# Sixteen column units of the input projection as eight pairs with seven quarter products each, in a stage ahead of the attention, and an attention with a lag of three head tiles

## The chip, the cores and the metric

The kernel runs on one core of a Trainium2 chip. The metric is device time in microseconds, taken as the median of several runs. The engines are TensorE (PE in the profile, with its weight loads as PEld), VectorE (DVE), ScalarE (ACT), GpSimd (POOL) and SyncE (SP, which issues most transfers here). Every engine takes its instructions in the order of the program.

## The reference

One layer of a streaming encoder, for 1024 prompt tokens and 64 sample tokens (1088 together, T in the code) with 1024 channels. Cut to what matters:

```python
h = rms_norm(x, norm_w) @ w_in                       # 1024 x 6144
sb_q, sb_k, sb_v, sb_z, cb_q, cb_k, cb_v, cb_z, g_sb, g_cb = split(h)
# stick-breaking attention, 8 heads of 64
w[t, s] = beta[t, s] * prod(1 - beta[t, j] for s < j < t)   # beta = sigmoid(q.k / 8)
o_sb = w @ v
# band attention: softmax(q.k / 8 + rel_bias) over 9 chunks of 64, q and k normalised per head
o_cb = softmax(...) @ v
b_sb = (o_sb * silu(sb_z)) @ w_proj_sb
b_cb = (o_cb * silu(cb_z)) @ w_proj_cb
y = x + (sigmoid(g_sb) * b_sb + sigmoid(g_cb) * b_cb) @ w_out
```

Keys and values of both branches are outputs too. All is float32. The kernel gets float32 accuracy out of a faster type: each operand is split into a high part and a low remainder, and a product is the sum of three: high by high, low by high, high by low.

## The kernel before

**Phase 1** (lines 150 to 408) normalises the input and transposes it into `xhl`, high and low parts with channels on partitions and tokens along the row. It then computes eight groups of 256 columns of the input projection (list `NB`) with tokens on partitions: the values of both branches and the queries and keys of the band branch. The matmuls are on line 357.

**Column units.** The other 32 blocks of 128 columns are units (`make_units`, line 120): stick-breaking keys and queries (4 + 4), the two SiLU gates (4 + 4), the two branch gates (8 + 8). `run_fill` (line 556) is a generator that issues one matmul of a unit at a time (line 563): for each of three chunks of tokens (384, 384 and 320) eight channel blocks by three products, 72 matmuls a unit. Weights of the next unit are split by `W.split`: `whi` on ACT (line 91), `wlo` on POOL (line 98). The results leave through `ev_k`, `ev_q`, `ev_silu` and `ev_act`. Keys and queries go by transfers from SBUF to SBUF to the place where the attention reads them (`place_k`, `place_q`).

**Attention** (lines 692 to 905) walks over 144 head tiles (`seq`): stick-breaking then band, four head pairs each, per pair the sample tile (t = 8) and eight tiles of 128 queries, two heads each. One step of the loop has these parts, in this order on PE: scores of head tile i (`qk`, lines 725 and 726), half of the step's fillers (`fill`, from `run_fill`), outputs of a finished pair of tiles (`av`, line 817), transposes of the weights of head tile i - LAG (`tr`, line 777), the other half of the fillers. ACT makes two sigmoids of the scores (`kp`, line 728, and `be`, line 729). DVE makes the weights of head tile i (`mid`): a scan of products over the keys (line 745) and a multiplication (line 746). The transposed weights leave PSUM by ACT (line 786) and DVE (line 788) in turn. The number of fillers of a step follows its number of keys; 22 units' worth less 48 matmuls are spread over the stick-breaking steps, and 746 matmuls over the band steps, the last of which belong to the first branch projection (`proj_units`, line 661). Ahead of the first step stand two units and 48 matmuls (the lead-in, lines 858 to 860).

**Merge and output** (phases 4 and 5) do the rest of the projections (line 661), the gated merge and the output projection (lines 986 to 992).

What sets the order is the program's text: the fillers' number per step, the lag, and how many buffers each tile has (`kp` 2, `be` 3, two PSUM tiles for transposes, three for scores).

## Time and profile before

| | us |
|---|---|
| median of three runs | 1036.61 (1036.37 to 1039.8) |
| span of the profiled execution | 1034.6 |
| phase 1 after its start, 19 to 231 us | 212 |
| lead-in, 231 to 267 us | 36 |
| stick-breaking attention, 267 to 633 us | 366 |
| band attention, 633 to 870 us | 237 |
| merge and output, 870 to 1035 us | 165 |

The span runs from the first to the last instruction of one profiled execution; that execution's own time is not given apart from it. The page has the engines' busy times, the chain of work that ended last, groups of instructions and DMA issues; an answer by stretches has the busy time of each engine in a stage, an answer on waits what an engine stood idle for. A matmul's duration in the trace covers its way through the array, and neighbours overlap; the distance between two starts is what it costs in a row.

### The profile page before, as it was taken

The numbers are of one execution on the slowest core, as the hardware profiler recorded it, in microseconds if no ns is written. First come the engines' busy times: TensorE is split into PE (matmuls) and PEld (weight loads), VectorE is DVE, ScalarE is ACT, GpSimd is POOL, SyncE is SP. The second block draws the span as 40 slices with busy tenths as digits, with TensorE's granted clock in tenths as the row PEclk, the third lists the DMA queues.
The fourth block names the chain that finished last, engine by engine and source line by source line (L and its number), as shares of the span: only waits on it lengthen the run. The fifth ranks groups of instructions, "written<-read, shape, count | busy, mean of one in ns | idle before, by whom it ended". The sixth has DMA issues, their size and how long they took to land.

```text
span 1034.6 us, 19354 instructions
## 1 busy us (share of the span) xinstructions
PE 1014.8 (98%) x7412; PEld 968.4 (94%) x7412; DVE 543.9 (53%) x1069; ACT 418.7 (40%) x942; POOL 255.2 (25%) x277
## 2 busy tenths in 40 slices
PE   6999999999999999999999999999999999999998
PEld 5999999999999989999999999998988898999998
DVE  5416656402476556657655645565557685674111
ACT  5534443212454435444444454444445433552000
POOL 3227666202221111212121111101103211453110
PEclk9999999999999999999999999999999999999999
DMA  7654453745547323723384354665576834554322
GB/s 237 213 187 151 163 191 128 267 136 165 160 112 192 96 69 102 206 60 95 92 211 122 107 144 131 165 169 161 162 204 185 224 92 139 187 163 149 101 93 71
DMA packets 159660, 155.23 MB, mean 150 GB/s; under 512 B 23184, under 2 KB 144912, under 8 KB 159440
## 3 DMA queue, kind: packets, MB, share of 16 engines
q1 hardware_dynamic: 142800, 136.17, 44.2%
q10 hardware_dynamic: 16768, 17.83, 5.7%
q8 instruction: 58, 0.95, 0.4%
q14 instruction: 34, 0.28, 0.1%
HBM read 90.77 MB, written 49.81 MB: 136 GB/s over the span
## 4 chain that ended last, share of the span: by engine, by line
PE 91%; SPq 3%; DMA 2%; DVE 1%; ACT 1%; issue 1%; POOL 0%; ACTq 0%; DVEq 0%
PE acc L563 33%; PE acc L357 18%; PE acc L661 9%; PE o L817 7%; PE pt L777 6%; PE z L726 3%; PE z L725 3%; PE acc L992 3%; PE acc L991 3%; PE acc L990 3%; SPq L49 2%; DMA wrawx<-in_w_in_dram 1%; PE pk L301 1%; PE pt L229 1%; DMA d_ccbT<-hc 1%
## 5 line engine op out<-in xcount | busy, mean ns | idle before, releaser
L563 PE MATMUL acc<-xh,whi 128*128 128x384 f32 (+1 forms) x768 | 255.5, 333 | 0.1
L563 PE MATMUL acc<-xh,wlo 128*128 128x384 f32 (+1 forms) x768 | 255.3, 332 | 0.0
L563 PE MATMUL acc<-xl,whi 128*128 128x384 f32 (+1 forms) x768 | 254.8, 332 | 0.0
L98 POOL TENSOR_TENSOR wlo<-wraw,whi 128x1024 fp32r<-128x1024 f32 x51 | 127.6, 2501 | 440.2 <-ACT whi L91 386.1
L563 PEld LDWEIGHTS acc<-xh,wlo 128*128 128x128 f32 x768 | 144.8, 189 | 1.3
L563 PEld LDWEIGHTS acc<-xl,whi 128*128 128x128 f32 x768 | 144.5, 188 | 1.3
L563 PEld LDWEIGHTS acc<-xh,whi 128*128 128x128 f32 x768 | 144.5, 188 | 1.2 <-ACT sg L550 0.3
L745 DVE TENSOR_TENSOR_SCAN kp<-kp,imp 64x576 f32<-64x576 f32 (+8 forms) x72 | 110.6, 1536 | 5.1 <-ACT kp L728 5.1
L735 ACT ACTIVATE be<-be,sm 128x640 f32<-128x640 f32 (+5 forms) x72 | 50.8, 706 | 106.6 <-DVE sm L731 106.4
L728 ACT ACTIVATE kp<-z 128x384 f32<-128x384 f32 (+6 forms) x112 | 53.8, 480 | 97.3 <-PE z L726 87.6
L777 PE MATMUL pt<-ident,be 128*128 128x128 f32 (+2 forms) x608 | 88.8, 270 | 0.9 <-DVE wT L788 0.6
L786 ACT ACTIVATE wT<-pt 128x512 f32<-128x512 f32 (+3 forms) x104 | 52.9, 509 | 82.5 <-PE pt L777 81.6
L788 DVE COPY wT<-pt 128x256 f32<-128x256 f32 (+3 forms) x104 | 46.0, 442 | 70.3 <-PE pt L777 69.9
L777 PEld LDWEIGHTS pt<-ident,be 128*128 128x128 f32 (+2 forms) x608 | 68.7, 139 | 11.6 <-issue 7.1
L357 PE MATMUL acc<-whi,xh 128*128 128x256 f32 x256 | 75.2, 296 | 0.0
L357 PE MATMUL acc<-wlo,xh 128*128 128x256 f32 x256 | 71.7, 282 | 0.0
L357 PE MATMUL acc<-whi,xl 128*128 128x256 f32 x256 | 71.5, 281 | 0.0
L357 PE MATMUL acc<-whix,xh 128*128 128x256 f32 x256 | 70.9, 279 | 0.0
L357 PE MATMUL acc<-whix,xl 128*128 128x256 f32 x256 | 70.6, 278 | 0.0
L91 ACT ACTIVATE whi<-wraw 128x1024 fp32r<-128x1024 f32 x52 | 55.0, 1059 | 38.4 <-DVE y L996 35.8
L357 PE MATMUL acc<-wlox,xh 128*128 128x256 f32 x256 | 70.5, 277 | 0.0
L746 DVE TENSOR_TENSOR be<-be,kp 64x576 f32<-64x576 f32 (+8 forms) x72 | 62.3, 865 | 8.8
(157 smaller groups left out, 2168.7 us busy)
## 6 DMA issues: line engine op xcount, KB each, us to landing
wraw<-in_w_in_dram SPq DMA_DIRECT2D x40, 512.0 KB, 4.9
sq<-hl SPq DMA_DIRECT2D x32, 192.0 KB, 4.5
sq<-d_qT SPq DMA_DIRECT2D x32, 192.0 KB, 3.6
xt<-in_x_prompt_dram SPq DMA_DIRECT2D x8, 512.0 KB, 5.6
wrawx<-in_w_in_dram SPq DMA_DIRECT2D x8, 512.0 KB, 4.3
d_kT<-hl SPq DMA_DIRECT2D x8, 512.0 KB, 4.7
d_qT<-hl SPq DMA_DIRECT2D x8, 512.0 KB, 4.8
ks<-d_kT SPq DMA_DIRECT2D x16, 256.0 KB, 4.6
```

What stands on the lines that cost most here:

```text
L91: A.activation(h, raw, AF.Copy)
L98: (eng or G).tensor_tensor(out=l, in0=raw, in1=h[:].bitcast(F32), op=OP.subtract)
L357: TE.matmul(ps, x, w, start=m == 0, stop=m == len(steps) - 1)
L563: TE.matmul(ps[:, :b - a], w[:, k], xk(x, k)[:, a:b], start=k == 0 and n == 0, stop=k == KT - 1 and n == 2)
L661: TE.matmul(ps[:, :n], w[:, p, cw], g[:, a:e], start=p == 0 and m == 0, stop=p == NPAIR - 1 and m == 2)
L728: A.activation(kp[:r, x:y], z[:r, :m], AF.Sigmoid, scale=-0.125)
L735: A.activation(be[:r, :n], be[:r, :n], AF.Exp, bias=kp[:r, j:j + 1], scale=-1.0, accum_out=kp[:r, 2:3])
L745: V.tensor_tensor_scan(kp[:r, n - 1::-1], kp[:r, n - 1::-1], im[:, ::-1], 0.0, op0=OP.mult, op1=OP.add)
L746: V.tensor_tensor(out=be[:r, :n], in0=be[:r, :n], in1=kp[:r, 1:n + 1], op=OP.mult)
L777: TE.transpose(pt[:kr, x, :r], be[:r, kb * 128:kb * 128 + kr], ident[:r, :r])
L786: A.activation(w[:, sl:sl + m, q0:q0 + r], pt[:, :m, :r], AF.Copy)
L817: TE.matmul(o[hd * 64:hd * 64 + 64, c0:c1], vv[:kr, kb, hd * 64:hd * 64 + 64], wT[b, p, j, hd, s // 4][:kr, s % 4, c0:c1], start=si == 0, ...
```

## The change

Sixteen units (stick-breaking keys and queries, both SiLU gates) leave the attention. They are taken as eight pairs of 128 + 128 columns. For a pair the weights are a 2 by 2 block matrix (two halves of the channels, two units) and the input is one too (two halves of the channels, two halves of the tokens). The eight products of quarters are replaced by seven products of sums and differences of quarters. The tokens in `xhl` are put in two halves of 544 (512 prompt and 32 sample tokens each), which are worked on in chunks of 256 and 288 columns.

- Phase 1: the sums of input quarters (`make_t`) are made one per token tile during the last weight groups, and split again into high and low parts. The groups of `NB` stand in another order, the key transposes follow one tile later, and the cache transposes are three tiles apart.
- New stage (lines 530 to 646 of the kernel after): 56 products, each 24 matmuls. The sums of weights are made on DVE (`presum`), their high parts on ACT and low parts on POOL (`prep`), five products ahead. The products accumulate in six PSUM banks, and DVE adds the intermediate sums. Keys and queries are stored to DRAM, and the attention loads them from there, as it did for the band branch.
- Attention: a lead-in of 144 filler matmuls with the first loads between them, 504 fillers in the stick-breaking steps, 684 in the band steps. The lag is three head tiles, `kp` has three buffers and `be` four. In the stick-breaking part three of four groups of transposed weights leave by ACT. The gated outputs that the first projection reads (`make_og`) are split in small steps between fillers.

```diff
+    pairs = []
+    for p in (0, 2):
+        pairs += [("k", 512 + 128 * p, p), ("q", 128 * p, p)]
+    for p in (0, 2):
+        pairs += [("silu", 1536 + 128 * p, d_z["sb"][p:p + 2]), ("silu", 3584 + 128 * p, d_z["cb"][p:p + 2])]
+    units = [("ev_act", 4096 + 128 * j, (AF.Sigmoid, d_g["sb"][j])) for j in range(KT)]
+    units += [("ev_act", 5120 + 128 * j, (AF.Copy, d_g["cb"][j])) for j in range(KT)]
...
+            def sub(a, b, k):
+                d = pool.tile([128, HF], F32, name="d")
+                V.tensor_tensor(out=d, in0=x(0, *a[:1], k, a[1]), in1=x(0, *b[:1], k, b[1]), op=OP.subtract)
+                V.tensor_tensor(out=d, in0=d, in1=x(1, *a[:1], k, a[1]), op=OP.add)
+                V.tensor_tensor(out=d, in0=d, in1=x(1, *b[:1], k, b[1]), op=OP.subtract)
+                return d
+            def less(h, c, d, k):
+                e = pool.tile([128, HF], F32, name="d")
+                V.tensor_tensor(out=e, in0=x(0, h, k, c), in1=d, op=OP.subtract)
+                V.tensor_tensor(out=e, in0=e, in1=x(1, h, k, c), op=OP.add)
+                return e
+            def sums_of(k):
+                d = sub((0, 1), (0, 0), k)
+                yield 0, k, d
+                d = less(1, 1, d, k)
+                yield 1, k, d
+                yield 3, k, less(1, 0, d, k)
+                yield 2, k, sub((1, 1), (0, 1), k)
...
+            if s == 1:
+                sums[1] = total(r1[:, :, b], r2[:, :, b], OP.add)
+                sums[2] = total(sums[1], r1[:, :, a], OP.subtract)
+            elif s == 4:
+                sums[3] = total(r1[:, :, a], r1[:, :, b], OP.subtract)
+                load_raw(2 * i + 3)
+            else:
+                sums[4] = total(r2[:, :, a], sums[2], OP.subtract)
...
+            A.activation(t[:, 0], src, AF.Copy)
+            G.tensor_tensor(out=t[:, 1], in0=src, in1=t[:, 0].bitcast(F32), op=OP.subtract)
...
+        LEAD, HB = 5, 4
...
+            h = up.tile([128, 2, 288], F32R, name="hl", bufs=HB)
+            A.activation(h[:, 0, :n], src[:, :n], AF.Copy)
+            V.tensor_tensor(out=h[:, 1, :n], in0=src[:, :n], in1=h[:, 0, :n].bitcast(F32), op=OP.subtract)
+            p = arg + w
+            dst = (d_kT if kind == "k" else d_qT)["sb"][p]
+            soon(0, lambda: stores(rdma, half, c, h[:, :, :n], dst[:]))
...
+        right = [lambda s: xhl[s][0][:, :, 0:HF], lambda s: tms[1][s], lambda s: tms[0][s],
+                 lambda s: xhl[s][1][:, :, 0:HF], lambda s: tms[2][s], lambda s: tms[3][s],
+                 lambda s: xhl[s][1][:, :, HF:T]]
+        BANK = "1231223"
...
+            for s in range(7):
+                n = 7 * i + s
+                prep(n + LEAD)
+                presum(n + LEAD + 1)
+                if n + LEAD == 7 * len(pairs) + 2:
+                    W.split(("u", 0))
+                if n + LEAD == 7 * len(pairs) + 1:
+                    load_unit(1)
+                step()
+                w = blk.pop(n)
+                for c, (a, b) in enumerate(XC):
+                    m = b - a
+                    if s < 3:
+                        bank[BANK[s], c] = psB.tile([128, 512], F32, name=f"b{BANK[s]}{c}")
+                    ps = bank[BANK[s], c]
+                    for k in range(4):
+                        for e, (hl_, x) in enumerate(((0, 0), (0, 1), (1, 0))):
+                            TE.matmul(ps[:, :m], w[:, hl_, k], right[s](x)[:, k, a:b], start=s < 3 and k == 0 and e == 0,
+                                      stop=k == 3 and e == 2, skip_group_check=s > 2)
+                    if s == 0:
+                        s1[c] = up.tile([128, 288], F32, name="s1")
+                        A.activation(s1[c][:, :m], ps[:, :m], AF.Copy)
+                    elif s in (1, 4):
+                        u = up.tile([128, 288], F32, name="u2" if s == 1 else "u3")
+                        (u2 if s == 1 else u3)[c] = u
+                        V.tensor_tensor(out=u[:, :m], in0=ps[:, :m], in1=s1[c][:, :m], op=OP.add)
+                    elif s == 3:
+                        emit(i, 0, 0, c, ps, True)
+                    elif s == 5:
+                        V.tensor_tensor(out=s1[c][:, :m], in0=ps[:, :m], in1=s1[c][:, :m], op=OP.add)
+                        emit(i, 1, 0, c, s1[c], False)
+                    elif s == 6:
+                        V.tensor_tensor(out=u2[c][:, :m], in0=ps[:, :m], in1=u2[c][:, :m], op=OP.add)
+                        emit(i, 0, 1, c, u2[c], False)
+                if s == 4:
+                    for c, (a, b) in enumerate(XC):
+                        m = b - a
+                        V.tensor_tensor(out=u3[c][:, :m], in0=bank["3", c][:, :m], in1=u3[c][:, :m], op=OP.add)
+                        emit(i, 1, 1, c, u3[c], False)
...     def fill(n):
+        n += owed[0]
+        owed[0] = 0
...
-        be = am.tile([128, NP], F32, name="be", bufs=3)
+        be = am.tile([128, NP], F32, name="be", bufs=4)
...
-            kp = ax.tile([128, NP + 2], F32, name="kp", bufs=2)
+            kp = ax.tile([128, NP + 2], F32, name="kp", bufs=3)
...
-                if flip[0] % 2:
+                if flip[0] % 2 or b == "sb" and flip[0] % 4:
...
-    load_v("sb", 0)
-    until(1)
-    fill(48)
-    FP = 170
-    n_sb = 72 * FILL_SB - 48
-    n_cb = 72 * (len(units) - 2 - FILL_SB) + FP
+    load_k("sb", 0, 1)
+    for f in (lambda: load_q("sb", 0, 3), lambda: load_k("sb", 0, 0), lambda: load_q("sb", 0, 0),
+              lambda: load_v("sb", 0), lambda: None, lambda: None):
+        fill(24)
+        flush()
+        f()
+    FP = 180
+    n_sb = 72 * 7
+    n_cb = 72 * (len(units) - 9) + FP
...
-    LAG = 2
+    LAG = 3
```

Three places show how the instructions stand. The first is PE at the end of phase 1. Before, the first unit follows (`xh`, `xl` are the input's high and low parts, `whi`, `wlo` the weights'):

```order
L357 MATMUL acc<-whix,xh_132 128x256
L357 MATMUL acc<-whix,xl_134 128x256
L357 MATMUL acc<-wlox,xh_132 128x256
L563 MATMUL acc<-xh_131,whi 128x384
L563 MATMUL acc<-xl_133,whi 128x384
L563 MATMUL acc<-xh_131,wlo 128x384
```

and after, the first product follows (`b` are its banks; high and low weights now share a tile):

```order
L451 MATMUL acc<-whix,xh_140 128x256
L451 MATMUL acc<-whix,xl_142 128x256
L451 MATMUL acc<-wlox,xh_140 128x256
L622 MATMUL b_3284<-xh_139,whi 128x256
L622 MATMUL b_3284<-xl_141,whi 128x256
L622 MATMUL b_3284<-xh_139,whi 128x256 x2
L622 MATMUL b_3284<-xl_141,whi 128x256
```

In the place of 72 matmuls a unit of 384 and 320 columns stand 24 a product of 256 and 288; the whole program has 2304 of line 563 before, and 1344 of line 622 and 1152 of line 759 after.

The second place is DVE beside the products of a key pair, in the new stage (`u` and `s` are the intermediate sums, `kf` a copy of the keys for their transposes, `ws` the sums of weights, `hl` the high and low parts):

```order
L387 TENSOR_TENSOR ws<-wraw 128x512
L387 TENSOR_TENSOR ws<-ws,wraw 128x512
L567 TENSOR_TENSOR hl<-b_3284,hl 128x256
L576 COPY kf<-b_3284 128x256
L567 TENSOR_TENSOR hl<-b_3299,hl 128x288
L576 COPY kf<-b_3299 128x288
L630 TENSOR_TENSOR u_3437<-b_3319,s_3297 128x256
L630 TENSOR_TENSOR u_3451<-b_3334,s_3312 128x288
L642 TENSOR_TENSOR u_3437<-b_3356,u_3437 128x256
L567 TENSOR_TENSOR hl<-u_3437,hl 128x256
```

Before, DVE had for a key unit only these two operations per chunk, here of the unit at the lead-in:

```order
L505 COPY kf<-acc 128x384
L495 TENSOR_TENSOR hl<-acc,hl 128x384
L505 COPY kf<-acc 128x384
L495 TENSOR_TENSOR hl<-acc,hl 128x384
L505 COPY kf<-acc 128x320
L495 TENSOR_TENSOR hl<-acc,hl 128x320
```

The evacuations moved out of the attention, and sums of weights and of products came to them.

The third place is DVE in the stick-breaking attention, at the tiles of 512 and 640 keys of the second head pair. Before:

```order
L745 SCALAR_TENSOR_TENSOR kp<-kp,imp 128x512
L746 TENSOR_TENSOR be<-be,kp 128x512
L788 COPY wT<-pt 128x3x128
L745 SCALAR_TENSOR_TENSOR kp<-kp,imp 128x512
L746 TENSOR_TENSOR be<-be,kp 128x512
L505 COPY kf<-acc 128x384
L495 TENSOR_TENSOR hl<-acc,hl 128x384
L745 SCALAR_TENSOR_TENSOR kp<-kp,imp 128x640
L746 TENSOR_TENSOR be<-be,kp 128x640
```

and after (the scan is the row with `kp` and `imp`, the copy of transposed weights the row with `wT`):

```order
L952 SCALAR_TENSOR_TENSOR kp<-kp,imp 128x512
L953 TENSOR_TENSOR be<-be,kp 128x512
L1027 TENSOR_TENSOR zt<-o,zt 128x256
L952 SCALAR_TENSOR_TENSOR kp<-kp,imp 128x512
L953 TENSOR_TENSOR be<-be,kp 128x512
L952 SCALAR_TENSOR_TENSOR kp<-kp,imp 128x640
L953 TENSOR_TENSOR be<-be,kp 128x640
L952 SCALAR_TENSOR_TENSOR kp<-kp,imp 128x640
L953 TENSOR_TENSOR be<-be,kp 128x640
L995 COPY wT<-pt 128x4x128
```

Scans and multiplications stand closer together: the units' evacuations are gone from between them, and of the copies of transposed weights 24 are left of 50.

426 lines of the change are left out of this document (259 added, 167 removed).

## The prediction

> **What bounds the kernel now.** I read the page's head and the chain first, then the busy time by stage, then what TensorE (PE) waited for.
>
> ```profile
> span 1034.6 us, 19354 instructions
> PE 1014.8 (98%) x7412; PEld 968.4 (94%) x7412; DVE 543.9 (53%) x1069; ACT 418.7 (40%) x942; POOL 255.2 (25%) x277
> PE 91%; SPq 3%; DMA 2%; DVE 1%; ACT 1%; issue 1%; POOL 0%; ACTq 0%; DVEq 0%
> 19.00:231.00 212.00, 210.76 (x1800) 209.79 (x1799) 94.33 (x202) 80.47 (x198) 94.08 (x101) 1.00 0.54 181
> 231.00:267.00 36.00, 35.62 (x219) 35.30 (x217) 6.83 (x12) 9.29 (x15) 8.11 (x6) 1.00 0.67 179
> 267.00:633.00 366.00, 365.88 (x2464) 343.90 (x2465) 220.47 (x261) 169.34 (x382) 60.48 (x91) 1.00 0.43 121
> 633.00:870.00 237.00, 234.90 (x1698) 213.16 (x1697) 149.06 (x469) 106.51 (x254) 38.00 (x34) 1.00 0.60 169
> 870.00:1035.00 165.00, 158.96 (x1191) 158.32 (x1190) 64.97 (x115) 42.51 (x78) 46.80 (x29) 1.00 0.41 130
> PE pt L229 <- DVE xn L218: 8.1, 2, 7.5
> PE acc L357 <- ACT whi L91: 2.2, 1, 2.2
> ```
>
> PE is busy 98% of the span and is 91% of the chain that ended last. The five stages (columns: length, then PE, weight load, VectorE (DVE), ScalarE (ACT), GpSimd (POOL), clock, DMA) are phase 1, the lead-in, the stick-breaking attention, the band attention, and the merge with the output projection. PE idles 0.1 us in the 366 us of the stick-breaking attention; what it waited for is mostly the start (8.1 us). So PE work that goes away shortens the kernel one for one, until another engine of the same stage is late. The nearest is DVE: 220 us of 366 there.
>
> **What the change takes from PE.** "Busy" overlaps neighbours, so the cost of one matmul is its spacing from start to start.
>
> ```profile
> 226.05 0.29 PE L357 MATMUL acc<-whix,xh 128*128 128x256 f32 x1
> ...
> 228.85 0.29 PE L357 MATMUL acc<-whix,xh 128*128 128x256 f32 x1
> 230.23 0.34 PE L563 MATMUL acc<-xh,whi 128*128 128x384 f32 x1
> ...
> 238.38 0.34 PE L563 MATMUL acc<-xh,wlo 128*128 128x384 f32 x1
> 238.56 0.49 PE L522 MATMUL pt<-ident,kf 128*128 128x128 f32 x3
> 238.80 0.39 PE L563 MATMUL acc<-xh,whi 128*128 128x320 f32 x1
> 239.03 0.30 PE L563 MATMUL acc<-xl,whi 128*128 128x320 f32 x1
> ...
> 242.25 0.31 PE L563 MATMUL acc<-xh,wlo 128*128 128x320 f32 x1
> 639.55 0.29 PE L725 MATMUL z<-kss,sqs 128*64 128x288 f32 x1
> ...
> 639.95 0.29 PE L726 MATMUL z<-kss,sqs 128*64 128x288 f32 x1
> ```
>
> A 384-column matmul takes (238.38 - 230.23) / 47 = 0.1734 us, a 320-column one (242.25 - 239.03) / 22 = 0.1464 us, a 256-column one (228.85 - 226.05) / 24 = 0.117 us, and a 288-column one (639.95 - 639.55) / 3 = 0.133 us. A column unit of before is 48 matmuls of 384 and 24 of 320 columns: 8.32 + 3.51 = 11.84 us. Sixteen of them are **189.4 us**. Of after, each of 8 pairs has 7 products of 12 matmuls of 256 and 12 of 288 columns: 12 x (0.117 + 0.133) = 3.0 us a product, 56 products, **168.0 us**. The change takes 21.4 us from PE. The key transposes become 40 instead of 36, at (238.80 - 238.56) / 3 = 0.08 us: 0.3 us, left out.
>
> The rule that speaks against this: the Trainium skill, page "TensorE: Matmul & The Clock Gate", section "Back-to-back issue gap", gives for a stream of weight load and matmul about 81 ns at 128 columns and 131 ns at 512. An estimate between these two figures of that page of the Trainium skill (98, 102, 106 and 114 ns at 256, 288, 320 and 384 columns) has the old units at 128 us and the products at 134 us, so that the change would cost 6 us. The trace does not agree with it (0.1734 us at 384 columns), and the sum goes by the trace.
>
> **What it adds on the other engines, stage by stage.**
>
> Phase 1. The 16 sums of input quarters are 40 DVE operations and 16 low-part subtractions of 544 columns, and 16 ACT copies; they stand one sum per token tile beside the last three weight groups. By the 576-column multiplication of 0.75 us quoted below the 56 operations are 42 us of DVE. Their cover is 19 tiles or more of 24 matmuls, 2.8 us each by the spacing, 53 us, in a phase where DVE is busy 94 of 212 us. I take 0; if the cover is gone, the second product waits for its quarter, some us once. The new order of weight groups, the later key transposes and the spread cache transposes touch waits that PE does not show; 0, bounds -1 and +2.
>
> The new stage. Each product needs a 512-column copy on ACT and a 512-column subtraction on POOL, each pair four sums on DVE, and evacuations.
>
> ```profile
> L98 POOL TENSOR_TENSOR wlo<-wraw,whi 128x1024 fp32r<-128x1024 f32 x51 | 127.6, 2501 | 440.2 <-ACT whi L91 386.1
> wraw<-in_w_in_dram SPq DMA_DIRECT2D x40, 512.0 KB, 4.9
> d_kT<-hl SPq DMA_DIRECT2D x8, 512.0 KB, 4.7
> ```
>
> POOL: half of 2.5 us, 7 times, 8.8 of a pair's 21 us. DVE has some 24 operations a pair of 0.3 to 0.6 us (the copies and evacuations below are 0.38 to 0.48 us), some 11 us. Weights are prepared five products (15 us) ahead, loads land in 4.9 us. PE accumulates again in a bank that DVE has just read: the sixth product starts its first half 1.6 us (12 x 0.133) after the fifth ended its own, and DVE's addition takes about 0.4 us. The staging ring has four tiles, so a store must land within about two products (6 us) against 4.7 us. All hides; what is left is the entry (weights that wait for memory of phase 1: 0.5 us of copy and 1.3 us of subtraction against the 6 us that two prepared products cover) and the exit. I take **+2 us**, bounds 0 and +12 (1.5 us a pair).
>
> The lead-in has 144 matmuls (24 us) instead of the first units. In it the queue on SP loads five pieces, each 4 to 5 us after issue, one after another; keys and queries now come back from DRAM, and the store of a filler that waits for ACT stands ahead of the next load. 24 us cover about 20: 0, bounds 0 and +5.
>
> The stick-breaking attention is where it is decided. It loses 1032 of 1536 filler matmuls (1032 x (2 x 0.1734 + 0.1464) / 3 = 169.6 us) and 27 transposes, so PE needs 366 - 169.6 - 2 = **194 us**. What DVE needs:
>
> ```profile
> L745 DVE TENSOR_TENSOR_SCAN kp<-kp,imp 64x576 f32<-64x576 f32 (+8 forms) x72 | 110.6, 1536 | 5.1 <-ACT kp L728 5.1
> L746 DVE TENSOR_TENSOR be<-be,kp 64x576 f32<-64x576 f32 (+8 forms) x71 | 61.1, 860 | 8.7
> L788 DVE COPY wT<-pt 128x256 f32<-128x256 f32 (+3 forms) x50 | 23.8, 476 | 54.5 <-PE pt L777 54.3
> L820 DVE TENSOR_TENSOR zt<-o,zt 128x256 f32<-128x256 f32 (+1 forms) x19 | 7.3, 383 | 41.9 <-PE o L817 32.6 <-PE acc L563 5.5 <-DMA zt<-d_zsb 3.7
> 345.44 2.28 DVE L745 TENSOR_TENSOR_SCAN kp<-kp,imp 128x1024 f32<-128x1024 f32 x1
> 347.86 1.23 DVE L746 TENSOR_TENSOR be<-be,kp 128x1024 f32<-128x1024 f32 x1
> 358.66 2.40 POOL L98 TENSOR_TENSOR wlo<-wraw,whi 128x1024 fp32r<-128x1024 f32 x1 [9.43 <-ACT whi L91]
> 359.63 2.64 DVE L745 TENSOR_TENSOR_SCAN kp<-kp,imp 64x576 f32<-64x576 f32 x1
> 362.37 0.75 DVE L746 TENSOR_TENSOR be<-be,kp 64x576 f32<-64x576 f32 x1
> 364.49 1.34 DVE L745 TENSOR_TENSOR_SCAN kp<-kp,imp 64x576 f32<-64x576 f32 x1
> 369.76 0.42 DVE L745 TENSOR_TENSOR_SCAN kp<-kp,imp 128x128 f32<-128x128 f32 x1
> 370.31 0.29 DVE L746 TENSOR_TENSOR be<-be,kp 128x128 f32<-128x128 f32 x1
> ```
>
> A step of scan and multiplication takes 2.42 + 1.23 = 3.65 us at 1024 keys and 0.55 + 0.29 = 0.84 us at 128, so 0.44 us + 3.14 ns a key; over the 72 steps with 41,472 keys 32 + 130 = 162 us, against 172 us busy now. The difference is POOL: the same scan is 2.64 us beside a split of weights and 1.34 us alone. Of 21 such splits 7 stay: 7 x 1.3 = 9 us. 24 copies instead of 50 are 11.5 us, the outputs 7.3 us. The sum is **190 us of DVE beside 194 us of PE**. ACT takes over 26 of the copies, but keeps fewer fillers:
>
> ```profile
> L728 ACT ACTIVATE kp<-z 128x384 f32<-128x384 f32 (+6 forms) x112 | 53.8, 480 | 97.3 <-PE z L726 87.6 <-issue 4.4 <-DVE be L746 3.7
> L729 ACT ACTIVATE be<-z 128x384 f32<-128x384 f32 (+6 forms) x112 | 54.0, 482 | 0.0
> ```
>
> 53.8 + 54 us and 76 copies at DVE's 0.48 us are 144 us, and the seven units left come on top, against 169 us busy today. So PE ends last by 4 us in 72 steps: DVE may idle only 0.06 us a step. It idles at the short tiles, where a step of PE is little over 1 us and a new scan must wait for ACT, about 1.5 us in each of four head pairs. A lag of three head tiles instead of two lets DVE run behind PE meanwhile, and the third buffer of kp makes that possible. I take **+4 us** (four times 1.5 us, less part of the margin), bounds 0 and +64 (below, the third rival).
>
> The band attention loses 62 fillers (10 us, already in the 189.4 us, as are the 48 of the lead-in) and has DVE busy 149 of 237 us; that leaves room. Where the two attentions meet, the biases wait for the last scan, now with less filler ahead: +1 us, bounds -1 and +4. The projection's inputs are made in small steps; PE does not wait there today, 0.
>
> **Sum.** 1034.6 - 21.4 + 2 + 4 + 1 = 1020.2 us of span. The median of the runs, 1036.6 us, is 2 us above the profiled span; I take that as what lies around it: **1022 us**.
>
> **Rivals.**
>
> 1. *DVE becomes the bound of the stick-breaking attention.* For it: 190 of 194 us. If DVE idles 15 us in its order (waits for ACT at short tiles, for transposes ahead of copies), the stage takes 205 us, 11 instead of 4 above PE's work: 1029 us. Against it: DVE's work per step is below PE's at every tile size but the shortest. Chance 0.20.
>
> 2. *The new stage stalls on its own support.* If the evacuation chain of every pair costs PE 1.5 us, 12 us instead of 2: 1032 us. For it: one ring of four tiles and stores of 4.7 us; against it: 11 us of DVE in 21. Chance 0.12.
>
> 3. *Slower: DVE keeps the waits that it has now in front of copies and outputs.* Its order is fixed, and a scan stands behind the copy of an earlier tile's transposes. Now it idles 54.5 us before 50 copies and 41.9 us before 19 outputs. With 24 copies and 19 outputs at the same 1.1 and 2.2 us each that would be 68 us, 258 us of DVE, +64; at half of it 224 us, +30 instead of +4, 1048 us. It decides from 25 us of idle time on (190 + 25 = 194 + 21). Against it: these waits are there because DVE is ahead of PE; once it is behind, the transposes are ready. Chance 0.09.
>
> 4. *A matmul has a fixed part.* If 288 columns cost what 320 do (0.1464) and 256 the 0.119 that the line through 384 and 320 columns gives, the products take 56 x 12 x 0.265 = 178 us and the change saves 11 us: 1032 us. For it: the 288-column row is a short run with another stationary width. Against it: 24 matmuls in a row at 0.117 us, with a new weight each. By the page of the Trainium skill named above it would even be a loss. Chance 0.05.
>
> That the work does not go away is excluded: of after 1152 fillers and 1344 product matmuls stand in the order, and 2304 of before.
>
> **Numbers.** The forecast, 1014 to 1027 us by its own bounds, has 0.54. From about 0.5% (5 us) on, a measurement of this kernel can tell a change. Faster by more than that, under 1031.4 us: all of the forecast, most of the first rival, half of the second: 0.76. Within: 0.15. Slower: the third rival, 0.09. The range reaches over the first, second and fourth rivals and down to no added wait (1014) less 1 to 2 us for spacings: 1012 to 1034 us, with the third rival and the tails, 0.2, left out.
>
> **What would show it.** Product matmuls of 256 columns 0.117 us apart and a new stage of 168 to 172 us; PE without waits in it. In the stick-breaking attention a length near 200 us, DVE over 90% busy, PE's waits a few us, before transposes. I am wrong if that stage passes 210 us, if PE waits in the new stage for copies or banks, or if the spacing is above 0.13 us.

## The result, and the profile after

| | before | after |
|---|---|---|
| median, us | 1036.49 (1035.1 to 1039.8) | **1179.62** (1176.95 to 1181.03) |
| span of the profiled execution | 1034.6 | 1177.2 |
| ratio, 95% interval | | **1.137** (1.135 to 1.140) |

The change makes the kernel 143 us slower, where 14 us faster had been forecast. The page's head, PE's row and the chain after:

```profile
span 1177.2 us, 20256 instructions
PE 1034.6 (88%) x7608; PEld 980.4 (83%) x7608; DVE 615.1 (52%) x1219; ACT 460.7 (39%) x1064; POOL 295.0 (25%) x321
PE 65%; DMA 14%; DVE 8%; SPq 6%; ACT 3%; issue 2%; POOL 1%; DVEq 0%; ACTq 0%; POOLq 0%
```

PE is 65% of the chain instead of 91%, and DMA is 14% instead of 2%. By stage (new stage, lead-in, stick-breaking attention, band attention, merge; columns as in the prediction: length, busy time of PE, PEld, DVE, ACT, POOL, granted clock, DMA share, GB/s):

```profile
233.00:413.00 180.00, 175.72 (x1388) 174.38 (x1388) 86.63 (x174) 69.21 (x159) 80.54 (x55) 0.99 0.44 134
413.00:437.00 24.00, 23.93 (x146) 23.61 (x145) 2.46 (x5) 3.72 (x7) 3.23 (x2) 1.00 0.28 86
437.00:730.00 293.00, 213.22 (x1414) 187.65 (x1413) 171.06 (x187) 139.60 (x338) 26.56 (x80) 0.85 0.41 118
730.00:1012.00 282.00, 238.49 (x1627) 214.10 (x1625) 143.30 (x466) 104.93 (x252) 32.41 (x32) 0.92 0.47 136
1012.00:1177.00 165.00, 161.28 (x1206) 160.54 (x1204) 65.22 (x116) 43.64 (x79) 49.61 (x30) 1.00 0.44 135
```

The new stage is 10 us above its forecast, the lead-in as forecast. The loss is in the two attentions: the stick-breaking one takes 293 us where 198 (194 + 4) were forecast, and the band one 282 us where it took 237 and 228 were forecast (237 - 10 + 1). PE stands idle 80 and 44 us in them. What PE waited for longest there (columns: total, times, longest):

```profile
PE pt L984 <- DVE wT L995: 41.5, 11, 13.3
PE z L932 <- DVE sm L938: 26.1, 4, 8.9
PE pt L984 <- DVE be L953: 23.1, 3, 11.2
PE z L932 <- ACT be L936: 19.1, 1, 19.1
```

So PE waits mostly for DVE. But DVE, the suspect of two rivals, is busy only 171 of 293 us, so its own work is no bound. Its longest waits for a transfer are:

```profile
DVE zt L1027 <- DMA zt<-d_zsb: 66.1, 7, 15.5
DVE zt L1027 <- DMA zt<-d_zcb: 49.8, 5, 12.9
```

DVE waits for `zt`, a gate tile of 128 KB, 116 us in twelve pieces. Scans, copies and outputs are in one order on DVE, so PE then waits for DVE. Why such a small load comes late is seen on SP, which issues the transfers (start, duration of the issue, line, transfer), and in the stretches of 2 us beside it:

```profile
472.31 0.59 SPq L1002 DMA_DIRECT2D zt<-d_zsb  x1
472.95 1.09 SPq L51 DMA_DIRECT2D ks<-d_ksbT  x2
475.33 6.74 SPq L675 DMA_DIRECT2D d_osb<-zt  x1
482.16 0.99 SPq L101 DMA_DIRECT2D wraw<-in_w_in_dram  x1
483.21 10.03 SPq L1002 DMA_DIRECT2D zt<-d_zsb  x1
```

```profile
478.00:480.00 2.00, 1.23 (x7) 1.19 (x8) 1.87 (x4) 1.28 (x3) 0.48 (x3) 1.00 0.13 53
480.00:482.00 2.00, 2.00 (x17) 1.42 (x15) 1.87 (x4) 1.17 (x3) 0.10 (x2) 1.00 0.13 53
488.00:490.00 2.00, 0.32 (x3) 0.05 (x1) 0.00 (x0) 0.00 (x0) 0.00 (x0) 1.00 0.13 53
490.00:492.00 2.00, 0.00 (x0) 0.00 (x0) 0.00 (x0) 0.00 (x0) 0.00 (x0) 0.68 0.13 53
```

At 472.95 two loads of prompt keys are issued, 512 KB each. Then the DMA share is 0.13, which is 2 of 16 engines, at 53 GB/s. 1 MB at 53 GB/s is 20 us. The store of outputs at 475.33 takes 6.74 us to be issued and the `zt` load at 483.21 takes 10.03, where the first one, before the keys, took 0.59. When the key loads are through, at about 493 by this sum, the issue ends; the chain of waits has `zt` from its issue to landing as one piece (start, duration):

```profile
483.21 15.44 DMA zt<-d_zsb
```

From 488 on PE does nothing until 501, and the clock falls to 0.68 of full speed in the last of these rows.

The held issue is not all, and mostly not what delays `zt`. Of the seven `zt` loads that come behind prompt keys, six are issued in 0.4 to 1.0 us and land 13.6 to 14.4 us after the start of their issue, like this one (the issue, and the operation of DVE that waited for it; the bracket has the idle time before and what ended it):

```profile
551.70 1.04 SPq L1002 DMA_DIRECT2D zt<-d_zsb  x1
565.38 0.42 DVE L1027 TENSOR_TENSOR zt<-o,zt 128x256 f32<-128x256 f32 x1 [15.52 <-DMA zt<-d_zsb]
```

The trace keeps the single landing records of each transfer, which none of the views prints. A `zt` load has sixteen. Of this one fourteen came within 2.8 us of its start and the last two after 13.6 us, at 565.3, right behind the last record of the keys at 564.9. So two of its sixteen parts stand behind the keys, and the issuer is held besides.

At the start of the stick-breaking attention the same happens to a store. The first pair's prompt keys are issued at 435.35, and behind them a store of a branch gate (`sg`), whose tile ACT needs again:

```profile
436.55 9.07 SPq L675 DMA_DIRECT2D d_gsb<-sg  x2
460.47 0.44 ACT L734 ACTIVATE sg<-acc 128x320 f32<-128x320 f32 x1 [21.55 <-DMA d_gsb<-sg]
461.54 0.50 PE L932 MATMUL z<-kss,sqs 128*64 128x288 f32 x1 [19.11 <-ACT be L936]
```

ACT takes up the scores only after that store has landed, and PE's next scores wait for ACT. This is PE's longest single wait, 19.1 us, and `zt` has no part in it.

Keys come through DRAM as the band branch's did before, but not in the same shape, and the band loads have the new shape too. The new `place_k` (lines 677 to 682 of the kernel after) loads the keys of a head with a pattern in DRAM whose outermost dimension counts two, high part and low part: `[[n, 2], [2 * n, 64], [1, o1 - o0]]`. The theory tested below, **theory A**: this count of two puts the whole transfer on two DMA engines. The Trainium skill states that very rule, on the page "DMA: Bandwidth & Descriptors", section "Why a DMA increments its semaphore by 16 and not by 1": a transfer runs on the largest number of engines, up to 16, that divides the slowest dimension (that is not one) of both its sides. The trace agrees (0.13 of 16 is two). The prediction did not price the loads by it. Against theory A stood first B and C, as the expectations give them, by which the shape of the loads is not the cause, and later D, that few large transfers with both parts in one are to blame.

### The profile page after: what moved, and what is told of

Its sections match the earlier page's. It is cut to its first block, busy times and chain, and to the rows that moved or that the text cites. A ratio compares the mean times of both kernels' runs of the same rounds, so it can differ in the third digit from the quotient of the medians.

```text
span 1177.2 us, 20256 instructions
## 1 busy us (share of the span) xinstructions
PE 1034.6 (88%) x7608; PEld 980.4 (83%) x7608; DVE 615.1 (52%) x1219; ACT 460.7 (39%) x1064; POOL 295.0 (25%) x321
## 4 chain that ended last, share of the span: by engine, by line
PE 65%; DMA 14%; DVE 8%; SPq 6%; ACT 3%; issue 2%; POOL 1%; DVEq 0%; ACTq 0%; POOLq 0%
PE acc L451 16%; PE b L622 13%; PE acc L865 8%; PE acc L759 7%; DMA zt<-d_zsb 5%; PE o L1024 4%; PE pt L984 4%; DVE kp L952 3%; SPq L51 3%; PE acc L1203 3%; PE acc L1202 3%; PE acc L1201 3%; SPq L675 2%; DVE be L953 2%; DMA ks<-d_kcbT 2%
## 5 line engine op out<-in xcount | busy, mean ns | idle before, releaser
L114 POOL TENSOR_TENSOR wlo<-wraw,whi 128x1024 fp32r<-128x1024 f32 x35 | 85.2, 2435 | 281.6 <-ACT whi L107 234.9
L759 PE MATMUL acc<-xh,wlo 128*128 128x384 f32 (+1 forms) x384 | 136.9, 357 | 1.4 <-POOL kp L923 1.4
L759 PE MATMUL acc<-xh,whi 128*128 128x384 f32 (+1 forms) x384 | 135.8, 354 | 1.2 <-ACT sg L734 1.1
L759 PE MATMUL acc<-xl,whi 128*128 128x384 f32 (+1 forms) x384 | 135.3, 352 | 0.0
L1027 DVE TENSOR_TENSOR zt<-o,zt 128x256 f32<-128x256 f32 (+1 forms) x40 | 15.4, 384 | 155.6 <-DMA zt<-d_zsb 66.1
L932 PE MATMUL z<-ks,sq 128*128 128x320 f32 (+4 forms) x192 | 65.9, 347 | 25.4 <-DVE sm L938 25.4
L759 PEld LDWEIGHTS acc<-xh,whi 128*128 128x128 f32 x384 | 77.7, 202 | 3.5 <-ACT sg L734 1.8
L759 PEld LDWEIGHTS acc<-xh,wlo 128*128 128x128 f32 x384 | 78.1, 203 | 3.0 <-POOL kp L923 1.8
L759 PEld LDWEIGHTS acc<-xl,whi 128*128 128x128 f32 x384 | 77.8, 202 | 1.0 <-issue 0.2
L1024 PE MATMUL o<-wT,vp 128*64 128x256 f32 (+1 forms) x608 | 67.1, 360 | 3.7 <-ACT wT L993 2.8
```

Of the source, the lines that this page charges most:

```text
L114: (eng or G).tensor_tensor(out=l, in0=raw, in1=h[:].bitcast(F32), op=OP.subtract)
L759: TE.matmul(ps[:, :b - a], w[:, k], xk(x, k)[:, a:b], start=k == 0 and n == 0, stop=k == KT - 1 and n == 2)
L932: TE.matmul(z[:r, :m], s[:, 2 * hd, q0:q0 + r], ks[:, hd, o + x:o + y], start=True, stop=False)
L1024: TE.matmul(o[hd * 64:hd * 64 + 64, c0:c1], vv[:kr, kb, hd * 64:hd * 64 + 64], wT[b, p, j, hd, s // 4][:kr, s % 4, c0:c1], start=si == 0, ...
```

## The experiments

Ratios are to the kernel before on the same chip, with 95% intervals. Lengths of attentions are from the first score of one to the first score of the next, or to the last output, and that of the new stage from its first product to its last. (The changed kernel has 291.4 and 283.6 us by this, against 293 and 282 in the rounder stretches above.)

**The loads undone, in both attentions and in one.** Each load of a head's keys becomes two of 64 partitions, so that the outermost count is 64.

```diff
         for hd in range(2):
-            rdma(dst[:, hd, a:b], bass.AP(tensor=src.tensor, offset=src.offset + hd * 128 * n + o0,
-                                          ap=[[n, 2], [2 * n, 64], [1, o1 - o0]]))
+            for s in range(2):
+                rdma(dst[64 * s:64 * s + 64, hd, a:b], src[64 * hd:64 * hd + 64, s, o0:o1])
```

> The kernel after, with one edit: every load of keys for the attention (place_k) is four transfers of 64 partitions each, as before the change, instead of two transfers whose outer dimension is 2 (high part, low part). Theory A, the outer dimension of 2 lets only two of the 16 DMA engines carry such a load (the DMA share stands at 0.13 = 2/16 with 50 to 53 GB/s in long stretches of the run after, 1 MB of keys then takes 20 us, and pieces of the transfers behind it wait in those two engines): both attentions lose their waits, the stick-breaking one takes 195 to 210 us instead of 293, the band one 225 to 235 instead of 282, the whole 1010 to 1030 us. Theory B, the vector engine bounds the stick-breaking attention: little changes, over 1140 us. Theory C, keys and queries of the stick-breaking branch through DRAM are too much for the queue on SP whatever their shape: over 1060 us.

Measured: **1031.89 us** (0.995, 0.994 to 0.997), 2 us above theory A's range. The stages of this kernel, from the new stage to the band attention, and its issues on SP in the first head pair (`kss` are cached and sample keys, `ks` prompt keys):

```profile
233.00:411.00 178.00, 174.05 (x1386) 172.74 (x1385) 87.64 (x174) 69.16 (x159) 80.03 (x55) 1.00 0.45 135
411.00:435.00 24.00, 24.00 (x149) 23.98 (x148) 2.62 (x6) 5.28 (x9) 5.74 (x6) 1.00 0.59 161
435.00:637.00 202.00, 195.44 (x1405) 172.97 (x1404) 170.34 (x186) 136.31 (x335) 23.84 (x76) 0.99 0.61 162
637.00:865.00 228.00, 224.84 (x1635) 203.35 (x1634) 145.32 (x468) 105.77 (x253) 33.23 (x32) 1.00 0.61 169
```

```profile
453.01 1.93 SPq L51 DMA_DIRECT2D kss<-d_csbT  x3
454.99 3.11 SPq L51 DMA_DIRECT2D kss<-d_ksbT  x4
458.19 0.53 SPq L675 DMA_DIRECT2D d_osb<-zt  x1
458.77 1.46 SPq L1001 DMA_DIRECT2D zt<-d_zsb  x1
```

Twice as many key loads are issued, and each issue takes 0.6 to 0.8 us; the `zt` load behind them takes 1.46 us and not 10. The attentions fall from 293 and 282 us to 202 and 228.

The same for the stick-breaking loads alone (the band loads stay at two rows):

> As the run before this one, but only the stick-breaking loads of keys are four transfers; the band loads stay two with an outer dimension of 2. Theory A: the stick-breaking attention is as short as there (195 to 210 us, though the first load for the band branch still falls into its last pair), the band attention stays long (270 to 285 us instead of 282): 1060 to 1090 us in all. Theory B: over 1140 us. Theory C: as in the run before this one, over 1060 us, with the loss in the stick-breaking part.

Measured: 1100.17 us (1.061, 1.059 to 1.063), 10 us above theory A's range. The stick-breaking attention takes 216.7 us, the band attention 281.8. The former's last head pair is 66.7 us long, against 52.0 in the first experiment, because the band's first keys are loaded in it; the expectation named that load and gave it no time. The stages answer one by one: the loads that are mended cost nothing more, those that are not cost what they did.

**The loads put into the kernel before.** Its band keys already came from DRAM, with four transfers of 64 partitions. They get the two-row pattern, nothing else.

```diff
-                place_k(alloc_k(("cb", p), 0), d_kT[p], 0, NP, 0, NP)
+                place_k2(alloc_k(("cb", p), 0), d_kT[p][:], 0, NP, 0, NP)
...
+    def place_k2(dst, src, o0, o1, a, b):
+        n = src.shape[-1]
+        for hd in range(2):
+            rdma(dst[:, hd, a:b], bass.AP(tensor=src.tensor, offset=src.offset + hd * 128 * n + o0,
+                                          ap=[[n, 2], [2 * n, 64], [1, o1 - o0]]))
```

> The kernel before, with only the loads of keys for the band attention as two transfers with an outer dimension of 2. Theory A: the band attention gets the waits of the run after, 30 to 50 us more than 237; 1065 to 1090 us in all. Theories B and C: as before, 1036 us within 5.

Measured: 1102.06 us (1.063, 1.061 to 1.065). The band attention goes from 235.8 to 290.9 us, the stick-breaking one is 10 us longer by the first band keys. The place is as expected, the size is 12 us above it. B and C fall: the same bytes, by the same way through DRAM, cost 65 us more in two transfers of two rows than in four of 64, in a kernel that has nothing else of the change.

**The count by itself.** Is it the count of the outermost dimension, or the number and make of the transfers (D)? A first kernel writes the four transfers as 4 x 16 rows:

```diff
-                rdma(dst[64 * s:64 * s + 64, hd, a:b], src[64 * hd:64 * hd + 64, s, o0:o1])
+                rdma(dst[64 * s:64 * s + 64, hd, a:b],
+                     bass.AP(tensor=src.tensor, offset=src.offset + (hd * 128 + s) * n + o0,
+                             ap=[[32 * n, 4], [2 * n, 16], [1, o1 - o0]]))
```

> The key loads are four transfers of 64 partitions as in the first experiment, but their access pattern in DRAM is written as 4 x 16 rows instead of 64, the same addresses. Theory A (the count of the outermost dimension sets over how many DMA engines a transfer is spread): four engines carry a key piece, so stretches show a DMA share of 0.25 and about 106 GB/s (twice the 53 of two engines) where only keys move; the two attentions lie between those of the first experiment and of the changed kernel: 1050 to 1100 us. Rival D (what cost the time in the changed kernel was that one transfer collects high and low parts, or that there were two transfers of 512 KB instead of four of 256 KB; the spelling of the dimensions is nothing): 1028 to 1036 us, as the first experiment.

Measured: 1034.47 us (0.998, 0.997 to 0.999). It tells nothing of A or D: the compiled transfers have one dimension of 64 rows, since 4 x 16 rows at one distance merge. (Its row step is 110 elements instead of 2176 as well, so the scores are of other data.) So two more kernels take the rows in an order that cannot merge, every fourth or every eighth first; k is 4 or 8. The channels of their keys stand in another order than those of the queries, so they time the loads and leave out the right scores:

```diff
+                             ap=[[2 * row, k], [2 * k * row, 64 // k], [1, m]]))
```

> Four transfers of 64 rows for each key piece as in the first experiment, but the rows of a half are fetched as 4 x 16 (every fourth row first), so that the pattern cannot be merged into 64 rows; the channels of the keys then stand in another order than those of the queries, and the scores are over mixed channels. Theory A (the outermost count is the number of DMA engines): four engines carry a piece, stretches with a DMA share near 0.25 and about 106 GB/s; 1 MB of keys takes 10 us instead of 20, half of what the other transfers behind it had to wait and less than half of what it cost: 1040 to 1090 us. Rival D (two large transfers or the joint high and low parts cost the time, not the count): 1028 to 1036 us.

> The same with 8 x 8 rows, scores over mixed channels again. Theory A: eight engines, about 212 GB/s, 1 MB of keys in 5 us, which the slack of the outputs mostly covers: 1030 to 1045 us, and below the run with 4 x 16 rows. Rival D: 1028 to 1036 us, no difference between the two.

Measured: 1072.07 us (1.034, 1.033 to 1.036) with four, 1044.61 us (1.007, 1.005 to 1.009) with eight. Stretches of 2 us with keys on the move, of the run with four and then of the run with eight:

```profile
528.00:530.00 2.00, 2.00 (x15) 1.97 (x14) 0.00 (x0) 2.00 (x6) 0.45 (x1) 1.00 0.25 104
530.00:532.00 2.00, 2.00 (x16) 1.96 (x14) 0.00 (x0) 2.00 (x8) 2.00 (x3) 1.00 0.26 107
```

```profile
514.00:516.00 2.00, 2.00 (x15) 1.97 (x14) 0.00 (x0) 2.00 (x5) 0.16 (x1) 1.00 0.50 125
516.00:518.00 2.00, 2.00 (x15) 1.96 (x14) 0.00 (x0) 2.00 (x8) 2.00 (x1) 1.00 0.54 146
```

The shares are 4 and 8 of 16. The rate does not follow in proportion: 125 and 146 GB/s in the rows with eight, where the expectation had 212; why stays open. The landing records count the same, and one more: a key load with two rows leaves 3, with four 5, with eight 9, and one with 64 or 128 rows leaves 16 (of the 3, 5 and 9 the first comes about 1 us after the issue, the others with the data). With the number of transfers, their bytes and their parts the same, the excess over the kernel of the first experiment is 40 us and 13 us; with two rows it was 148. Against D stands also the opposite change: keys stored in the order of the load, so that a piece is one transfer of 1 MB with 128 rows outermost.

```diff
-        for hd in range(2):
-            for s in range(2):
-                rdma(dst[64 * s:64 * s + 64, hd, a:b], src[64 * hd:64 * hd + 64, s, o0:o1])
+        rdma(dst[:, :, a:b], src[:, :, o0:o1])
...
+                for hd in range(2):
+                    soon(0, lambda hd=hd: stores(rdma, half, c, h[64 * hd:64 * hd + 64, :, :n],
+                                                 dst[:, hd].rearrange("(s d) n -> d s n", s=2)))
```

> The keys lie in DRAM in the order in which they are loaded (high and low part, then channel, outermost), so that a key piece is one transfer with 128 rows in its outermost dimension (1 MB for the 1024 prompt keys); the stores are two transfers of 64 rows instead of one of 128. Theory A (outermost count): all 16 engines carry it, no stretch with a DMA share of 0.13, 1026 to 1034 us. Rival D (few large transfers that collect both parts are what makes others wait): a transfer of 1 MB holds up outputs at least as the two of 512 KB did, over 1080 us.

Measured: 1035.05 us (0.999, 0.998 to 1.000), 1 us above A's range and far from D's. The stick-breaking attention is 198.5 us, 3 less than with four transfers, but the new stage, with two stores for each key piece instead of one, is 181.7 us instead of 178.0. (That the stores cost this is not shown.) So the largest transfer does no harm, and D falls.

**Another queue.** Is it SP, which stands in its issues, or the two DMA engines as such? The two-row loads of the changed kernel go out from ACT's queue:

```diff
-            rdma(dst[:, hd, a:b], bass.AP(tensor=src.tensor, offset=src.offset + hd * 128 * n + o0,
+            A.dma_start(dst[:, hd, a:b].bitcast(F32),
```

> The changed kernel with its key loads, still two transfers with an outermost count of 2, issued from ScalarE's queue instead of SyncE's, and nothing else. Theory A1 (later transfers wait because they stand behind the key pieces in the same queue of the two engines): on another queue the two engines take turns between the pieces, outputs and stores get through, and most of the 148 us above the first experiment goes: 1040 to 1110 us. Theory A2 (the two engines as such are what is shared, and a piece that comes beside keys waits for them on whichever queue): 1140 to 1185 us, with the waits for zt as long as in the changed kernel.

Measured: **1247.57 us** (1.204, 1.201 to 1.207), outside both ranges. DVE now waits 16.2 us for `zt` from DMA instead of 116. That alone does not show that other transfers get through, because ACT now stands in the issues, DVE and SP come to a stop behind it, and few gate tiles are issued beside prompt keys:

```profile
632.66 0.51 ACTq L681 DMA_DIRECT2D ks<-d_ksbT  x1
634.72 6.72 ACTq L681 DMA_DIRECT2D kss<-d_csbT  x1
641.48 9.75 ACTq L681 DMA_DIRECT2D kss<-d_csbT  x1
651.27 10.28 ACTq L681 DMA_DIRECT2D kss<-d_ksbT  x2
661.60 0.38 ACT L994 ACTIVATE wT<-pt 128x256 f32<-128x256 f32 x1 [25.93 <-issue]
```

ACT computes nothing for 26 us here and, unlike SP, it has sigmoids, exponentials and copies to do. That is the price that neither theory had. Where a gate tile does come beside keys, it still waits. This one is issued on SP 3 us after the first of the prompt keys on ACT's queue:

```profile
473.15 0.59 SPq L1003 DMA_DIRECT2D zt<-d_zsb  x1
483.11 0.23 DVE L1028 TENSOR_TENSOR zt<-o,zt 128x64 f32<-128x64 f32 x1 [16.18 <-DMA zt<-d_zsb]
```

Fourteen of its sixteen landing records come within 2.4 us and the last two after 9.7 and 9.9, while the keys land until 497. The next `zt`, issued at 485.07, has fourteen within 3.6 us and the last after 15.3 us, as late as in the changed kernel. So A1 is right that the issues are no longer in `zt`'s way (0.3 and 0.6 us), but A2 is right that the two engines are shared by both queues: what comes beside keys waits there on either. Neither had the size.

**What is left between the first experiment and the forecast.** It is 10 us above 1022. Three runs are about parts of it, and one about the lag, a step of the prediction:

```diff
-    LAG = 3
+    LAG = 2
```

> The first of these four with a lag of two head tiles instead of three. If the vector engine's margin of 4 us in the stick-breaking attention is as thin as predicted, the shorter lag costs 5 to 25 us there; if the margin is larger or the order of the engines leaves slack, under 3 us.

Measured: 1042.16 us (1.006, 1.004 to 1.008); the stick-breaking attention is 212.6 us instead of 201.7, with this on top of PE's waits (in the first experiment the same row is 3.6 us):

```profile
PE pt L983 <- DVE be L952: 13.5, 6, 5.5
```

The third head tile of lag is worth about 10 us, within the 5 to 25 expected. Then the copies of the stick-breaking attention, all on ACT:

```diff
-                if flip[0] % 2 or b == "sb" and flip[0] % 4:
+                if flip[0] % 2 or b == "sb":
```

> The first experiment with all copies of transposed weights of the stick-breaking attention on ScalarE, none on VectorE. Theory (VectorE's narrow margin costs the 7 us between that stage's 202 us and its 195 us of TensorE work): VectorE loses 11 us, the stage becomes 3 to 6 us shorter, the kernel 1026 to 1029 us. Rival (the margin is not it: TensorE waits there at the first steps of each head pair, and a copy on ScalarE stands behind two evaluations of scores): the stage stays within 2 us or becomes up to 6 us longer, the kernel 1031 to 1038 us.

Measured: **1029.87 us** (0.993, 0.992 to 0.995); the attention takes 199.1 us. The 2.6 us less are a little under the range, so DVE's margin is part of the 7 us and not all. This is the lowest median of the study, but its interval overlaps that of the first experiment: the gain rests on the stage's length, in one profiled execution of each kernel (and 198.3 us in the last run of this section, which has the same copies). Next, the kernel before with phase 1's second weight half on the other side of memory:

```diff
+        natx = ph.enter_context(tc.tile_pool(name="natx", bufs=2, side="right"))
...
-            W.load((i, h), wpool if h == 0 else p1,
+            W.load((i, h), wpool if h == 0 else natx,
```

> The kernel before with the second half of phase 1's weights in a pool of its own on the other side of memory, as the changed kernel has it, and nothing else. Theory (the place of the moving operand costs 4 ns a matmul in those matmuls): the first column unit starts 2 to 4 us later than 230.23 us and the kernel takes 1038 to 1041 us. Rival (the 2.9 us come from the changed order of weight groups or from the input sums that run beside them): the first unit starts within 1 us of 230.2 and the kernel is within 1 us of before.

Measured: 1040.1 us (1.004, 1.002 to 1.005); the first unit starts at 233.56 instead of 230.23. That is phase 1's loss, since in the first experiment the new stage starts at 233.17. Last, the copies on ACT together with the keys' sample rows in another tile:

```diff
-                ko = up.tile([128, 2, 128], F32, name="ko", bufs=3)
+                ko = up.tile([128, 3, 128], F32, name="ko", bufs=2)
...
-                    kos = up.tile([32, 128], F32, name="kos", bufs=1)
+                    kos = ko[:32, 2]
```

> The first experiment with all copies of the stick-breaking attention on ScalarE, and with the evacuated sample rows of the keys in the tile of the other rows (ko, three slots, two buffers) in place of their own single buffer. Theory: the copies bring the 2 us that they brought alone, and the four key pairs lose the waits for the single buffer, 2 to 4 us in sum in the waits of TensorE before the transposes' bank, so the new stage takes 173.5 to 176.5 us instead of 178.0: 1025 to 1028.5 us. Rival (the pairs are longer by their transposes and what stands behind these in order): 1029 to 1031 us.

Measured: 1032.28 us (0.996, 0.995 to 0.998). (More buffers for these rows alone do not fit: with three, their pool needs 25.875 KB a partition where 25.34 are left, so that kernel has no time.) The waits of PE in the key pairs are as before, and the theory of the single buffer falls:

```profile
PE acc L583 <- ACT ko L589: 4.3, 3, 2.5
```

(4.0 us in the first experiment.) What ends them stays open, and so does whether this run is really above the one with the copies alone: the intervals touch at 0.995.

## Why the prediction was wrong

**The step that failed** is the price of the key loads. The prediction has it in the lead-in: "the queue on SP loads five pieces, each 4 to 5 us after issue, one after another; keys and queries now come back from DRAM". The 4 to 5 us are from rows of transfers with 128 or 64 rows outermost. The new loads have two, and the two pieces of a pair's prompt keys land 22 to 24 us after their first issue, by the landing records of the changed kernel. And in the two attentions, where each head pair loads the next pair's keys, the sum has no term for them: a cost put at nothing without a reason. The runs put it at 148 us, the changed kernel less the first experiment, of which some 145 are in the two attentions. The lead-in itself, where the prediction saw the danger, takes its 24 us with either shape. This row of before and this one of the first experiment (kilobytes each, then the median time to landing in us) are what the old shape costs:

```profile
ks<-d_kT SPq DMA_DIRECT2D x16, 256.0 KB, 4.6
```

```profile
ks<-d_ksbT SPq DMA_DIRECT2D x16, 256.0 KB, 4.6
```

None of the four rivals had this mechanism; the one on the slower side was about DVE's own waits. The whole diff has it: `place_k` goes from four transfers to two, and the pattern begins with a two.

Of the signs named beforehand, the stick-breaking attention passed 210 us by far, and PE's waits in it were for DVE; that these came from DMA the signs did not foresee. PE also waits for copies in the new stage, another of the signs, but only 4 us. With the loads mended the other steps can be read.

- **Products: right.** In the first experiment the product that starts a pair without keys comes at 348.01 us, and the next pair's at 369.09, 21.08 us for seven products of 3.0 us. The first rows of its first two products and of the next pair:

```profile
348.01 0.27 PE L622 MATMUL b<-xh,whi 128*128 128x256 f32 x1
...
351.02 0.28 PE L622 MATMUL b<-t1h,wlo 128*128 128x256 f32 x1
...
369.09 0.27 PE L622 MATMUL b<-xh,whi 128*128 128x256 f32 x1
```

A product takes 351.02 - 348.01 = 3.01 us. The Trainium skill's figures that were weighed against this change (page "TensorE: Matmul & The Clock Gate", section "Back-to-back issue gap", 81 ns at 128 columns and 131 ns at 512) give 2.4 us a product by the prediction's estimate between them. The trace does not agree with them here. Rival 4, with 12 x 0.265 = 3.18 us, does not hold either.

- **New stage: undersized.** +2 us (0 to 12) against 178.0 - 168 = 10. The four pairs of gates are as planned; the two pairs of keys and the two of queries take 9.4 us more, of which 40 transposes of 0.08 us are 3.2 and waits about 4; the rest is not traced to a cause. 36 of the transposes were there before and only move here from the fillers, so they are no loss of the kernel.
- **Phase 1: outside its bounds** (-1 to +2), +2.9 us (first product at 233.17 against first unit at 230.23). The prediction did not mention the new place of the weights, which alone gives +3.3 us in the kernel before (233.56 against 230.23).
- **Lead-in:** 24.0 us as forecast, with two rows and with 64.
- **Stick-breaking attention:** 201.7 us against 198; PE works 195.4 (194 forecast). The 190 us of DVE were too much. The rows that they were added up from sum to 178 us here (100.8 + 59.0 for scans and multiplications, 11.2 copies, 7.2 outputs), and because neighbours overlap, as on PE, DVE is busy only 170 us of 202. So it is not "over 90% busy", the margin was wider than 4 us, and rival 1 did not come about as it was put. Yet the stage is 2.6 us shorter with DVE's last copies on ACT, so its order costs PE a little.
- **The lag: right** in its sense, about 10 us; the prediction gave it no number.
- **Clock.** In the changed kernel PE is busy 213 + 238 us in the attentions and 195 + 225 in the first experiment for the same matmuls, with a granted clock of 0.85 and 0.92 against 0.99 and 1.00. So some 31 of the 148 us are PE running slower during and after idle stretches (the clock is still 0.50 from 464 to 468 us, when PE is busy again after its wait of 19 us), as a consequence of the waits.

The algebra saves on PE what it promised. What remains of the change is 0.5% faster than before with four transfers, and 0.7% with ACT's copies as well.

## What to carry to other kernels

Price a transfer by its shape: read the count of the outermost dimension first, and bytes after that. When a diff merges several transfers into one with a hand-written pattern, look for a small leading dimension. And look at what stands behind it: a small transfer spread over all engines is as late as its parts on the busy ones, and the queue's issuer is held. So the loss appears at transfers that have nothing to do with it, here the load of a 128 KB gate tile and the store of a branch gate. Another queue does not free them of it, and a queue whose issuer has work of its own makes it worse.

## What the runs showed of the hardware that was not expected

- The time against the outermost count, with the same four transfers (4 and 8 with the rows in another order): 4 rows 1072 us, 8 rows 1045, 64 rows 1032 (and 2 rows, in half as many transfers, 1180). Two engines moved 53 GB/s, four 97 to 107, and eight 125 and 146 in the rows above.
- Small transfers beside keys on two engines have fourteen of their sixteen landing records within 4 us of the end of their issue and two more 4 to 14 us later: fourteen gate tiles and outputs in the changed kernel, with the keys on the same queue, and five with the keys on ACT's.
- A transfer's issue can take 10 us, on SP and on ACT, while key pieces stand ahead in the queue; on ACT such issues, one after another, stopped its computing for 26 us.
- The moving operand's place in memory changed the kernel before by 3 to 4 us in 1037: matmuls on the second half's weights have a mean of 283 ns instead of 278, some 5 ns in 768 matmuls. The grouped row of one of the three products, in the kernel before and then with `natx`:

```profile
L357 PE MATMUL acc<-whix,xl 128*128 128x256 f32 x253 | 69.8, 278 | 0.0
```

```profile
L358 PE MATMUL acc<-whix,xl 128*128 128x256 f32 x248 | 69.7, 283 | 0.0
```

  Whether it is the side or the address within it stays open.
